# A hybrid decoder layer on one core: memory's square sums five chunks later, mix-out's first three blocks in turn by halves, token sums of x dropped between uses

## The chip, the cores and the metric

The kernel runs on one core of a Trainium2 chip. The metric is device time in microseconds (us), the median of several executions. One more execution was profiled; every trace number in this document is from such a profiled execution, counted from the start of its span.

Engines are named as in the profile: PE is TensorE (matmul), PEld its weight load, DVE is VectorE, ACT is ScalarE, POOL is GpSimd, and SP is SyncE, whose queue issues all large loads and all transposes by DMA.

## The reference, cut to what matters

One decoder layer over 256 tokens of width 2048, in float32. Two token mixers run side by side and are merged with sigmoid gates; then come cross-attention to 256 memory tokens, a gated FFN with a short convolution, and a final norm.

```python
hn = rmsnorm(h, norm_mix_w)
q, k, v, g_ret, xr, yr, g_a, g_b = split(hn @ w_in)
ret = head_groupnorm(chunkwise_retention(rotary(q), rotary(k) * dk**-0.5, v))
ret_out = silu(g_ret) * ret
hr = rg_lru(causal_dwconv(xr))                    # gates from two block-diagonal products
rnn_out = gelu(yr) * hr
merged = sigmoid(g_a) * (ret_out @ w_proj_ret) + sigmoid(g_b) * (rnn_out @ w_proj_rnn)
h = h + merged @ w_mix_out
mem_n = rmsnorm(mem, norm_mem_w)
h = h + cross_attention(rmsnorm(h, norm_xa_w), mem_n)
h = h + (silu(gate) * val) @ ffn_w_down           # gate, val = conv(rmsnorm(h, norm_ffn_w) @ ffn_w_up)
return rmsnorm(h, final_norm_w)
```

## The kernel before

**Products in two parts.** Each float32 operand is split into a high part `hi` (rounded for TensorE's fast float32 kind) and a low part `lo`. A product takes three matmuls: high by high, low by high, high by low. All are issued on L245, so the profile has one line for every matmul and tells them apart by their tiles: `acc` and `sm` are PSUM tiles (three of two banks and two of one bank), `s` is a split pair of 256 tokens, `ts` are token sums (below), `rp` the parts of the recurrence's gate products.

**Weights as one stream.** All weights lie in one array `wall`, in the order in which the kernel uses them. `weight_plan` lists the products, `pieces` cuts each into chunks, and `weight_stream` sets the order of the chunks. An ordinary product of 512 columns (`steps_n`) has chunks of 4 x 128 rows, 24 matmuls each. `prefetch` loads a chunk (1 MB) into one of three `raw` buffers, ScalarE casts its `hi` (L343), VectorE subtracts for `lo` (L344), each 1024 columns at a time, into six buffers of each kind: parts of three ordinary chunks. In the program's order the parts of two chunks ahead are made before a chunk's matmuls.

**Pairs with seven products.** `steps_pair` makes two blocks of 512 columns at once, in chunks of 2 x 128 rows by 1024 columns. An ordinary chunk has 24 matmuls. In the chunks named by `seven` (chunks 2 and 5, unless told otherwise), a scheme of seven products in place of eight takes 21 matmuls; it needs four additions of weights on VectorE (L364), seven parts in place of eight, and sums of the tokens' blocks (`sums_of`, tile `ts`). These sums are kept in the dictionary `token_sums` and used again when the same tokens meet another pair. A sum holds one of the 29 buffers of the pool `big` from its making to its last use. `SEVEN` is the default pair of chunks; `SEVEN_O` and `SEVEN_U` are other choices.

**Deferred work.** `later(n, fn)` runs `fn` in the program's order after n + 1 more chunks. `by_dma(rows, then, wait)` turns token rows into feature rows: ScalarE copies the rows into planes `pl` (L546), the SP queue issues two transposes into `pt` (L547), and after `wait` chunks ScalarE joins them into `f` (L559) and calls `then`.

**Order.** A scheduler orders each engine's instructions by priority and by when it expects buffers of a pool to be free; an engine then works through its own list in order. Matmuls are pinned to the program's order, and so are the square sums in `sum_squares` (L634).

**The stages that the change touches**, in order of time:

1. Two groups of heads: queries, keys, values and the retention gate. In the second group the values are one pair, `both("w_in", O_V + 1024)`, then the gate pair.
2. Four blocks of the recurrence, each a product for x and one for y. `recur` makes two gate products into PSUM tiles `sm` and empties them with two tanh (L889, L890); the second writes into `ti`, a buffer of `big`. `gelu_y` makes rnn's features, splits them (L582, L583) and, for features 2 and 5, makes their token sums at once from the unsplit source (L448 to L456).
3. The merge: two ordinary products for the second gate, a pair of `w_proj_rnn`, a pair for the gate, a pair of `w_proj_rnn`, then the first gate's pairs and those of `w_proj_ret`. Each merged block of 512 features goes through `by_dma` and `turn_merged` into two split pairs of the list `merged` (8 in all).
4. Mix-out (`residual`): four ordinary products `w_mix_out`, 16 chunks, each over all of `merged`. The rows of x (`hrow`) and of memory (`mnat`), eight loads of half a megabyte, are issued ahead of it. Blocks 0 and 1 run three chunks each, then the last chunk of each, then block 2, then block 3. `memory_steps` puts the four square sums of memory after the first four chunks.
5. Keys and queries of the cross-attention.

```python
def in_turn(products):
    return [c for o in products for c in o[:-1]] + [o[-1] for o in products]
```

Of the kernel before, what the change touches and what calls it, by code (L numbers as in the profile page):

```python
# [17 lines left out]
P = 128  # L18
D = 2048
S = 256  # L20
NT = D // P
# [7 lines left out]
BW = 512  # L29
KC = 4  # L30
# [11 lines left out]
SEVEN = (2, 5)  # L42
SEVEN_O = (3, 5)
SEVEN_U = (4,)

O_Q, O_K, O_V, O_G = 0, 1024, 2048, 4096
O_XR, O_YR, O_GA, O_GB = 6144, 8192, 10240, 12288
# [26 lines left out]
def weight_plan():  # L74

    plan = []
    for g in range(2):
        keys = [("w_in", 0, NT, c + g * BW) for c in (O_Q, O_K)]
        values = [("w_in", 0, NT, O_V + b * BW) for b in range(2)]
        plan += keys + [both("w_in", O_V + 1024)] if g else [keys[0], values[0], keys[1], values[1]]  # L80
        plan.append(both("w_in", O_G + g * 1024))
    for b in range(4):
        plan += [("w_in", 0, NT, c + b * BW) for c in (O_XR, O_YR)]
    plan += [("w_in", 0, NT, O_GB + b * BW) for b in range(2)] + [both("w_proj_rnn", 0)]
    plan += [both("w_in", O_GB + 1024), both("w_proj_rnn", 1024)]
    plan += [both(w, c + b * BW) for w, c in (("w_in", O_GA), ("w_proj_ret", 0)) for b in (0, 2)]
    plan += [("w_mix_out", 0, NT, b * BW) for b in range(4)]
    plan += [(w, 0, NT, b * BW) for b in range(4) for w in ("xa_w_k", "xa_w_q")]
    plan += [("xa_w_v", 0, NT, b * BW) for b in range(4)]
    plan += [both("xa_w_o", 0, SEVEN_O)] + [("xa_w_o", 0, NT, b * BW) for b in (2, 3)]  # L90
    for kind, *a in ff_plan():
        if kind == "down" and sum(a) < NF // 4:
            plan += [both("ffn_w_down", b * BW, SEVEN, a[0] * BW, 4 * a[1]) for b in (0, 2)]
        elif kind == "down":
            plan += [("ffn_w_down", a[0] * BW, 4 * a[1], b * BW) for b in range(4)]
        else:
            plan.append(both("ffn_w_up", a[0] * BW, SEVEN_U, apart=FF))
    return plan
# [28 lines left out]
    return [c for o in products for c in o[:-1]] + [o[-1] for o in products]  # L127


def weight_stream():  # L130

    out = [
        [(w, row + k * P, n, (*c[:2], k // KH in c[2]) if isinstance(c, tuple) else c) for k, n in pieces(i, nk, c)]
        for i, (w, row, nk, c) in enumerate(weight_plan())
    ]
    out[:2] = [[one for pair in zip(*out[:2]) for one in pair]]
    out[-4:-1] = [in_turn(out[-4:-1])]
    i = [c[0][0] for c in out].index("w_mix_out")
    out[i : i + 2] = [in_turn(out[i : i + 2])]
    return [one for chunks in out for one in chunks]  # L140


# [17 lines left out]
def hybrid_layer(  # L160
# [646 lines left out]
    for g in range(2):  # L807
        dec = big([P, 4, S], s="dec")
        vs, turned = [], ([], [])
        for b, o in enumerate((O_Q, O_K)):  # L810

            def rotate_both(f, o=turned[b]):
                o.append(rotated(f[:, 0:2, :]))
                later(0, lambda: o.append(rotated(f[:, 2:4, :])))

            a = gemm_n("w_in", 0, xs, NT, o + g * BW) if g + b else q0
            turned_rows(a, rs0, rotate_both, 2 - b if g + b else 3, g + b > 0)
            if b == 1:
                sp.dma_start(
                    out=dec,  # L820
                    in_=consts[:, C_DEC + g * 4 * S : C_DEC + (g + 1) * 4 * S].rearrange("p (h s) -> p h s", s=S),
                )
            if g == 0:
                v = gemm_n("w_in", 0, xs, NT, O_V + b * BW) if b else ended(v_steps)
                vs.append(split_rows(v, rs0))
        if g == 1:
            vs += [split_rows(v, rs0) for v in pair("w_in", 0, xs, NT, O_V + 1024, O_V + 1024 + BW)]
        qr, kr = turned
        gates = []
        c = O_G + g * 1024  # L830
        for a in pair("w_in", 0, xs, NT, c, c + BW):
            t = big([P, 2, BW], s="gate")
            for tt in range(2):
                act.activation(t[:, tt, :], a[:, tt, :], AF.Tanh, scale=half_rs0[:, tt : tt + 1])
            dve.scalar_tensor_tensor(out=a, in0=t, scalar=1.0, in1=a, op0=ALU.add, op1=ALU.mult)
            gates.append(a)
        retain(g, qr, kr, vs, dec, gates)


    lam = pb[:, 0:16]  # L840
# [70 lines left out]
    for b in range(4):  # L911
        rgw = big([P, 2, 4, P], s="rgw")
        for i, src in enumerate((rg_w_a, rg_w_x)):
            sp.dma_start(out=rgw[:, i], in_=src[0, 4 * b : 4 * b + 4].rearrange("g i j -> i g j"))
        xr, wparts = {}, []
        later(2, lambda wparts=wparts, rgw=rgw: wparts.extend(parts_of(rgw, pool.tensor_copy, pool)))

        def conv_x(f, b=b, xr=xr, wparts=wparts):
            xr[0] = big([P, 4, S], s="xr")
            for j in range(4):  # L920
                t = 4 * b + j
                z, y = f[:, j, :], xr[0][:, j, :]
                act.activation(y, z, AF.Identity, scale=p_cw(3, t), bias=p_cb(t))
                for s in range(1, 4):
                    dve.scalar_tensor_tensor(  # L925
                        out=y[:, s:S], in0=z[:, 0 : S - s], scalar=p_cw(3 - s, t), in1=y[:, s:S],
                        op0=ALU.mult, op1=ALU.add,
                    )

            three, xparts = [], parts_of(xr[0], act.copy, dve)  # L930

            def both(pr):
                if pr == 0:
                    three.extend(big([P, 4, S], s=n) for n in ("aa", "tt", "ti"))
                recur(b, wparts, xparts, xr[0], pr, *three)

            for pr in range(2):
                later(RG_WAIT + pr, lambda pr=pr: both(pr))

        def gelu_y(f, xr=xr):  # L940
            for pr in range(2):
                y = f[:, 2 * pr : 2 * pr + 2, :]
                y2, th = tmp("y2"), tmp("yt")
                act.activation(y2, y, AF.Square)
                dve.tensor_scalar(out=y2, in0=y2, scalar1=0.044715 * K0, scalar2=K0, op0=ALU.mult, op1=ALU.add)
                dve.tensor_tensor(out=y2, in0=y2, in1=y, op=ALU.mult)
                act.activation(th, y2, AF.Tanh)
                dve.scalar_tensor_tensor(out=y, in0=th, scalar=1.0, in1=y, op0=ALU.add, op1=ALU.mult)
            for pr in range(2):
                o = tmp("rn")  # L950
                cs = slice(2 * pr, 2 * pr + 2)
                dve.tensor_tensor(out=o, in0=xr[0][:, cs, :], in1=f[:, cs, :], op=ALU.mult)
                with_sums(rnn, SEVEN, o, 0.5)

        turned_rows(gemm_n("w_in", 0, xs, NT, O_XR + b * BW), rs0, conv_x)
        turned_rows(gemm_n("w_in", 0, xs, NT, O_YR + b * BW), rs0, gelu_y, 6)


# [11 lines left out]
        for pr in range(2):  # L970
            merged.append(split_pair(f[:, 2 * pr : 2 * pr + 2, :], 0.5))

    ts = [tanh_rows(big([P, 2, BW], s="sig"), gemm_n("w_in", 0, xs, NT, O_GB + b * BW)) for b in range(2)]
    mb = []
    for b in (0, 2):
        if b:
            ts = [tanh_rows(a, a) for a in pair("w_in", 0, xs, NT, O_GB + b * BW, O_GB + (b + 1) * BW)]
# [8 lines left out]
    for b in (0, 2):  # L986
        for i, m in enumerate(pair("w_proj_ret", 0, ret, NT, b * BW, (b + 1) * BW)):
            gated(ts[b + i], m)
            dve.tensor_add(m, m, mb[b + i])  # L989
            by_dma(m, turn_merged, 1 + 2 * (b + i == 3))  # L990


    hrow = [load_rows(x, c) for c in range(4)]
# [3 lines left out]
    def residual(w, st, out, wcol, steps=None):  # L997

        ss = sums()
        products = [steps_n(w, 0, st, NT, b * BW) for b in range(4)]  # L1000
        sources = []
        for b in range(4):
            if steps:
                steps(b)
                if b == 0:
                    for one in products[:2]:
                        for _ in range(NT // KC - 1):
                            next(one)
            elif b == 0:
                sources += pair(w, 0, st, NT, 0, BW, SEVEN_O)  # L1010
            h = hrow[b]
            dve.tensor_add(h, h, sources.pop(0) if sources else ended(products[b]))
            by_dma(h, lambda f, b=b: turn(f, b, out, wcol), 1 + (b == 1), b == 3 and steps is None)
            if b < 2:
                later(2 + b, lambda h=h, b=b: squares(h, ss, b))
            else:
                squares(h, ss, b)
        return ss
# [15 lines left out]
    def memory_steps(b):  # L1034
        if b == 0:
            ss = sums()[:, :, 0:2]
            for c in range(4):
                later(c, lambda c=c: sum_squares(mnat[c], ss, c))
            later(4, lambda: rsms.append(rstd_rows(ss)))
        if b == 2:  # L1040
            ms.load(2)
            for k2 in range(4):
# [257 lines left out]
```

## Time and profile before

| | before |
|---|---|
| time, median of 3 runs | 2010.1 us (2009.51 to 2012.91) |
| profiled execution: time, span | 2011.37 us, 2009.4 us |
| TensorE busy | 1971.7 us |
| VectorE busy | 1564.5 us |
| ScalarE busy | 1370.1 us |
| mean granted TensorE clock | 0.993 |
| read from HBM | 388.39 MB, 194 GB/s over the span |

A busy engine in the page is one that executes; its wait for a semaphore counts as idle. The view of waits names, for each line, what ended the idle time before it. A timeline merges neighbouring instructions of one kind: start, time from the first start to the last end, count, and in brackets the idle time before. A row of the windows view gives a stretch, its length, and the busy time of each engine with the count of its instructions; then come the granted TensorE clock, the share of the DMA engines and the rate in GB/s.

### The profile page before, as it was taken

Reading aid. Unit: us, or ns where it says so; the run is one execution under the profiler, and the core shown is the slowest. Engines: PE = TensorE matmul, PEld = TensorE weight load, DVE = VectorE, ACT = ScalarE, POOL = GpSimd, SP = SyncE. Lnnn points to the kernel's source line nnn. Section 1 sums busy time; section 2 is a strip of 40 time slices with the busy share of each in tenths; the row PEclk is TensorE's granted clock in tenths of the full one; section 3 lists DMA queues with packets and bytes.
Section 4 is the critical chain, followed back from the end, with each engine's and each line's share of the span. In section 5 each row is a group of like instructions: output and inputs, shape, how many; then the busy total and the mean of one; then the engine's idle time right before and its main releaser. Section 6 shows DMA issues by size and latency. Waiting matters only on the chain.

```text
span 2009.4 us, 24019 instructions
## 1 busy us (share of the span) xinstructions
PE 1971.7 (98%) x8831; PEld 1635.7 (81%) x8831; DVE 1564.5 (78%) x2044; ACT 1370.1 (68%) x1671; POOL 25.4 (1%) x25
## 2 busy tenths in 40 slices
PE   9999999998999999699999999999999999999998
PEld 8888788887888888588888888888888888888887
DVE  6887987898788888557546568678889868899686
ACT  6666658987645656568666666877877477874683
POOL 0000001000000000000000000000000000000000
PEclk9999999999999999899999999999999999999999
DMA  8756566666465465868666665756666656666673
GB/s 329 234 212 176 207 223 199 199 202 206 169 229 189 170 228 189 272 209 255 216 199 210 198 194 200 235 199 212 208 223 212 235 189 218 204 223 223 221 238 119
DMA packets 197190, 425.62 MB, mean 212 GB/s; under 512 B 142032, under 2 KB 146640, under 8 KB 152016
## 3 DMA queue, kind: packets, MB, share of 16 engines
q1 hardware_dynamic: 197072, 424.09, 63.2%
q8 instruction: 69, 1.13, 0.2%
q14 instruction: 49, 0.40, 0.1%
HBM read 388.39 MB, written 2.10 MB: 194 GB/s over the span
## 4 chain that ended last, share of the span: by engine, by line
PE 92%; DVE 3%; ACT 2%; issue 1%; DMA 1%; SPq 0%; POOL 0%; POOLq 0%; DVEq 0%; ACTq 0%
PE acc L245 67%; PE sm L245 25%; DVE lo L344 1%; ACT hi L343 1%; ACT f L559 0%; DMA nat<-in_mem 0%; ACT pl L546 0%; DVE tb L728 0%; DVE xr L925 0%; PE warm L242 0%; DVE rows L572 0%; DMA pt<-pl 0%; DVE ta L732 0%; DVE raw L364 0%; DVE fv L1127 0%
## 5 line engine op out<-in xcount | busy, mean ns | idle before, releaser
L245 PE MATMUL acc<-hi,s 128*128 128x512 f32 (+1 forms) x3974 | 1221.9, 389 | 17.2 <-ACT s L582 17.1
L344 DVE TENSOR_TENSOR lo<-raw,hi 128x1024 fp32r<-128x1024 f32 (+1 forms) x796 | 933.4, 1197 | 337.2 <-ACT hi L343 328.4
L343 ACT CAST hi<-raw 128x1024 fp32r<-128x1024 f32 (+1 forms) x796 | 792.4, 1023 | 419.0 <-PE acc L245 145.5
L245 PEld LDWEIGHTS acc<-hi,s 128*128 128x128 f32 x3974 | 745.5, 188 | 170.5 <-ACT s L582 17.6
L245 PE MATMUL acc<-lo,s 128*128 128x512 f32 (+1 forms) x1987 | 772.1, 389 | 1.7 <-DVE lo L344 1.7
L245 PEld LDWEIGHTS acc<-lo,s 128*128 128x128 f32 x1987 | 374.1, 188 | 79.4 <-DVE lo L344 2.5
L245 PE MATMUL sm<-hi,s 128*128 128x512 f32 x1336 | 411.3, 389 | 0.0
L245 PEld LDWEIGHTS sm<-hi,s 128*128 128x128 f32 x1336 | 250.8, 188 | 52.0
L245 PE MATMUL sm<-lo,s 128*128 128x512 f32 x668 | 260.0, 389 | 0.0
L559 ACT COPY f<-pt 128x1024 uint16<-128x1024 uint16 x128 | 167.0, 1353 | 35.5 <-DMA pt<-pl 33.9
L245 PEld LDWEIGHTS sm<-lo,s 128*128 128x128 f32 x668 | 125.4, 188 | 26.0
L364 DVE TENSOR_TENSOR raw<-raw 128x512 f32<-128x512 f32 x164 | 113.1, 690 | 2.5
L245 PE MATMUL acc<-hi,ts 128*128 128x512 f32 x246 | 76.8, 394 | 1.4 <-ACT hi L343 1.4
L546 ACT COPY pl<-rows 128x1024 uint16<-128x1024 uint16 x56 | 55.7, 1042 | 21.6 <-DVE rows L570 12.2
L546 ACT COPY pl<-o 128x1024 uint16<-128x1024 uint16 x52 | 51.6, 1039 | 6.4 <-DVE o L989 6.4
L245 PEld LDWEIGHTS acc<-hi,ts 128*128 128x128 f32 x246 | 46.3, 189 | 11.7 <-ACT hi L343 2.2
L245 PE MATMUL acc<-lo,ts 128*128 128x512 f32 x123 | 49.0, 398 | 1.1 <-DVE lo L344 1.1
L1127 DVE SCALAR_TENSOR_TENSOR fv<-f,pf,fv 128x255 f32<-128x255 f32 (+1 forms) x88 | 38.6, 482 | 0.0
L524 DVE TENSOR_TENSOR o<-o,acc 128x512 f32<-128x512 f32 x52 | 33.4, 687 | 6.1 <-PE acc L245 6.1
L1127 DVE SCALAR_TENSOR_TENSOR fg<-f,pf,fg 128x255 f32<-128x255 f32 (+1 forms) x88 | 35.8, 479 | 0.0
L514 DVE TENSOR_TENSOR o<-o,acc 128x512 f32<-128x512 f32 x52 | 35.6, 685 | 0.0
L524 DVE TENSOR_TENSOR o<-o,sm 128x512 f32<-128x512 f32 x52 | 34.4, 688 | 0.3 <-PE sm L245 0.2
(193 smaller groups left out, 1011.1 us busy)
## 6 DMA issues: line engine op xcount, KB each, us to landing
raw<-in_wall SPq DMA_DIRECT2D x352, 1024.0 KB, 4.8
nat<-in_x SPq DMA_DIRECT2D x8, 512.0 KB, 9.2
raw<-in_wall SPq DMA_DIRECT2D x7, 512.0 KB, 5.9
pt<-pl SPq DMA_TRANSPOSE x128, 3.3
nat<-in_mem SPq DMA_DIRECT2D x4, 512.0 KB, 8.8
xt<-in_x_t SPq DMA_DIRECT2D x3, 512.0 KB, 8.9
xt<-in_mem_t SPq DMA_DIRECT2D x3, 512.0 KB, 5.5
dec<-in_consts SPq DMA_DIRECT2D x2, 512.0 KB, 4.4
```

Source lines behind the costliest of these rows:

```text
L245: tc.keep_in_program_order(pe.matmul(*a, **k))
L343: act.copy(hi[:, cs], src[:, cs])
L344: dve.tensor_tensor(out=lo[:, cs], in0=src[:, cs], in1=hi[:, cs].bitcast(F32), op=ALU.subtract)
L364: dve.tensor_tensor(out=o, in0=a, in1=b, op=ALU.add)
L514: dve.tensor_tensor(out=o, in0=a, in1=b, op=op)
L524: dve.tensor_tensor(out=o, in0=o, in1=banks[a], op=ALU.add)
L546: act.copy(planes[:, tt], words[:, tt])
L559: act.copy(halves_[:, :, :, cs], turned_[:, :, :, cs])
L1127: dve.scalar_tensor_tensor(out=y[:, s:S], in0=z[:, j, 0 : S - s], scalar=pf[:, 2 - s, t : t + 1], in1=y[:, s:S], op0=ALU.mult, op1=ALU.add,)
```

## The change

- `SEVEN_V = (5,)`: the second group's value pair uses the seven-product scheme in chunk 5 alone. Chunk 2 becomes an ordinary chunk.
- `token_sums.clear()` after the two groups of heads: the sums of x made there are not kept; the gate pairs of the merge make them again.
- `gelu_y` only splits. The token sums of features 2 and 5 of rnn are made by `later` after the first of the merge's ordinary gate products, from the split parts (one more addition each).
- Mix-out's blocks 0, 1 and 2 run two chunks each, then their other two chunks each (`by_halves`); block 3 follows as before. The weight stream is laid out in the same order.
- The fourth merged block is joined one chunk earlier.
- Memory's square sums come after chunks 6 to 9 in place of 1 to 4, and their root after chunk 10.

```diff
+SEVEN_V = (5,)
...
-        plan += keys + [both("w_in", O_V + 1024)] if g else [keys[0], values[0], keys[1], values[1]]
+        plan += keys + [both("w_in", O_V + 1024, SEVEN_V)] if g else [keys[0], values[0], keys[1], values[1]]
...
+def by_halves(products):
+
+    return [c for part in (slice(0, 2), slice(2, 4)) for o in products for c in o[part]]
...
-    out[i : i + 2] = [in_turn(out[i : i + 2])]
+    out[i : i + 3] = [by_halves(out[i : i + 3])]
...
-            vs += [split_rows(v, rs0) for v in pair("w_in", 0, xs, NT, O_V + 1024, O_V + 1024 + BW)]
+            vs += [split_rows(v, rs0) for v in pair("w_in", 0, xs, NT, O_V + 1024, O_V + 1024 + BW, SEVEN_V)]
...
+    token_sums.clear()
...
-                with_sums(rnn, SEVEN, o, 0.5)
+                rnn.append(split_pair(o, 0.5))
...
-    ts = [tanh_rows(big([P, 2, BW], s="sig"), gemm_n("w_in", 0, xs, NT, O_GB + b * BW)) for b in range(2)]
-    mb = []
+    ts, mb = [], []
+    for b in range(2):
+        ts.append(tanh_rows(big([P, 2, BW], s="sig"), gemm_n("w_in", 0, xs, NT, O_GB + b * BW)))
+        if b == 0:
+            for i, k2 in enumerate(SEVEN):
+                later(1 + 2 * i, lambda k2=k2: sums_of(rnn[k2]))
...
-            by_dma(m, turn_merged, 1 + 2 * (b + i == 3))
+            by_dma(m, turn_merged, 1 + (b + i == 3))
...
-                    for one in products[:2]:
-                        for _ in range(NT // KC - 1):
+                    for one in products[:3]:
+                        for _ in range(2):
                             next(one)
...
-                later(c, lambda c=c: sum_squares(mnat[c], ss, c))
-            later(4, lambda: rsms.append(rstd_rows(ss)))
+                later(5 + c, lambda c=c: sum_squares(mnat[c], ss, c))
+            later(9, lambda: rsms.append(rstd_rows(ss)))
```

## The prediction

> **What bounds the kernel now.** I read the page first, then what TensorE waits for, then the stages around its waits as timelines.
>
> ```profile
> span 2009.4 us, 24019 instructions
> PE 1971.7 (98%) x8831; PEld 1635.7 (81%) x8831; DVE 1564.5 (78%) x2044; ACT 1370.1 (68%) x1671; POOL 25.4 (1%) x25
> PE 92%; DVE 3%; ACT 2%; issue 1%; DMA 1%; SPq 0%; POOL 0%; POOLq 0%; DVEq 0%; ACTq 0%
> ...
> L344 DVE TENSOR_TENSOR lo<-raw,hi 128x1024 fp32r<-128x1024 f32 (+1 forms) x796 | 933.4, 1197 | 337.2 <-ACT hi L343 328.4
> L343 ACT CAST hi<-raw 128x1024 fp32r<-128x1024 f32 (+1 forms) x796 | 792.4, 1023 | 419.0 <-PE acc L245 145.5
> ...
> L364 DVE TENSOR_TENSOR raw<-raw 128x512 f32<-128x512 f32 x164 | 113.1, 690 | 2.5
> ```
>
> TensorE carries 92% of the chain that ended last and is idle for only 2009.4 - 1971.7 = 37.7 us. Work taken off another engine is worth something only if it closes one of those holes, or the slow stretch behind it. This is the list of the holes:
>
> ```profile
> PE acc L245 <- ACT s L582: 17.1, 1, 17.1
> PE sm L245 <- ACT ti L890: 8.1, 2, 6.6
> PE acc L245 <- DVE lo L344: 2.8, 4, 1.0
> PE acc L245 <- ACT hi L343: 1.4, 1, 1.4
> ```
>
> One wait of 17.1 us, two on L890 and five small ones. The change touches the places of the first two rows, and of part of the others.
>
> **Mix-out (first part of the change).** Here are TensorE's stretch before the hole (chain of waits), its first matmuls behind it (timeline) and the stretch that they begin (chain), then ScalarE and the SP queue over the same time.
>
> ```profile
> 817.60 10.67 PE acc L245 x47
> ...
> 845.62 1.52 PE L245 MATMUL acc<-hi,s 128*128 128x512 f32 x2 [17.14 <-ACT s L582]
> ...
> 845.62 59.52 PE acc L245 x251
> ```
>
> ```profile
> 828.34 1.04 ACT L343 CAST hi<-raw 128x1024 fp32r<-128x1024 f32 x1 [0.32 <-PE acc L245]
> 841.36 1.06 ACT L634 ACTIVATE nat<-nat 128x1024 f32<-128x1024 f32 x1 [11.97 <-DMA nat<-in_mem]
> ...
> 842.41 2.50 ACT L559 COPY f<-pt 128x1024 uint16<-128x1024 uint16 x2
> 844.94 1.15 ACT L582 ACTIVATE s<-f 128x512 fp32r<-128x512 f32 x2
> ```
>
> ```profile
> 825.52 0.40 SPq L216 DMA_DIRECT2D raw<-in_wall  x1
> 826.02 5.04 SPq L547 DMA_TRANSPOSE pt<-pl  x2
> 831.12 2.11 SPq L212 DMA_DIRECT2D nat<-in_x  x4
> 833.33 2.35 SPq L216 DMA_DIRECT2D nat<-in_mem  x4
> 835.78 36.71 SPq L216 DMA_DIRECT2D raw<-in_wall  x6
> ...
> DMA to landing us min/median/max: 8.0/9.6/13.0
> ```
>
> A mix-out chunk is 24 matmuls. 10.67 / 47 = 0.227 us each, so 5.45 us a chunk. TensorE did two chunks of block 0 (merged pairs 0 to 3), then needed pair 4. Its turned rows were to be copied and split by ScalarE, but the pinned square sum of memory (L634) stood ahead and waited 11.97 us for its load, which is the fifth of eight half-megabyte loads issued at 831 to 836. The hole ends when L634, the two copies (2.50) and the split (1.15) are done.
>
> After the change two things hold. By the instruction order that the changed program builds to, no L634 stands ahead of the copies: the four come after the casts of the tenth to twelfth chunks. And TensorE has six chunks (two of each of three blocks) that need pairs 0 to 3 alone: 6 x 5.45 = 32.7, from 817.6 to 850.3.
>
> When are pairs 4 to 7 there? ScalarE's next two instructions are now the casts of the sixth chunk. They wait for the buffers of the third, whose first half is free after 18 of 24 matmuls: 828.3 + 4.1 = 832.4, the second at 833.8; the cast ends by 834.8. Its weights were issued at 825.52, ahead of the eight loads. Then come two copies and two splits, twice: 2 x (2.50 + 1.15) = 7.3, so 842.1, and about 1.3 more for VectorE's low parts: 843.4, 7 us before need.
>
> What is late next is the seventh chunk's weights, queued behind the eight loads. They are issued at 835.78 and land at most 13.0 later (last row above): 848.8. Cast and subtraction (1023 and 1197 ns, L343 and L344) end at 851.0, while TensorE wants the high part at 850.3 and the low part 0.45 later. That leaves 0 to 0.4 us of waiting; I take 0.4.
>
> The stretch behind the hole is slow at its start: its 251 matmuls take 59.52 us where 251 x 0.227 = 57.0, so 2.5 more. The stage can give 17.1 + 2.5 = 19.6; I take **-19.2**. The square sums now fall among the casts of chunks 10 to 12, where ScalarE has room or not (a rival below). They issue no DMA, and the loads keep their places in the SP queue. What waits for the sums, the scaling of the first key block, comes after mix-out.
>
> **Recurrence (token sums dropped, sums of rnn later).**
>
> ```profile
> 478.48 1.60 PE L245 MATMUL sm<-rp,rp 128*128 128x256 f32 x12
> ...
> 492.13 2.93 PE L245 MATMUL sm<-rp,rp 128*128 128x256 f32 x12 [6.58 <-ACT ti L890]
> ```
>
> ```profile
> 482.82 0.64 ACT L455 ACTIVATE ts<-tq 128x512 fp32r<-128x512 f32 x1 [2.77 <-DVE tq L450]
> ...
> 485.02 1.98 ACT L546 COPY pl<-rows 128x1024 uint16<-128x1024 uint16 x2
> 486.91 1.99 ACT L343 CAST hi<-raw 128x1024 fp32r<-128x1024 f32 x2
> 491.60 0.84 ACT L890 ACTIVATE ti<-sm,h 128x256 f32<-128x256 f32 x2 [2.71 <-DMA pt<-pl]
> ...
> 480.70 0.42 DVE L448 TENSOR_TENSOR tq<-rn 128x256 f32<-128x256 f32 x1
> ...
> 483.84 1.40 DVE L572 TENSOR_SCALAR rows<-acc,ro 128x512 f32<-128x512 f32 x2
> 485.16 0.68 DVE L456 SCALAR_TENSOR_TENSOR ts<-tq,ts 128x512 fp32r<-128x512 f32 x1
> ```
>
> The second gate product pair needs the PSUM tiles that L889 and L890 empty. L890 waited for a transpose: its output `ti` is one of the 29 buffers of the pool `big`, all taken, and the next one to come free was the planes that the transpose reads. Dropping x's token sums after the second head group gives back two of the 29 for all four recurrence blocks, and the sums of rnn 2 and 5 are not yet made, which is one more in the third block and two in the fourth. In the built order of the changed program the fourth block's `ti` waits for no DMA. The four VectorE steps of the sum and L455 go too, so the rows of L572 start near 479.6 instead of 483.84. ScalarE's planes follow (2.0), then two casts (2.0) and the two tanh pairs (1.7): from 480.3 they end at 486.0, the first PSUM tile free near 485.2. TensorE wants it at 485.4. The hole gives 6.58, the half-speed products 2.93 - 1.60 = 1.33, the matmuls after them 0.2. The other hole on this line is 8.1 - 6.6 = 1.5 us in the third block, where ScalarE waited for the same kind of sum. Together 9.6; I take **-9.1**, with 0.5 left over.
>
> **V pair of the second head group (SEVEN_V).**
>
> ```profile
> 200.19 0.50 PE L245 MATMUL acc<-lo,ts 128*128 128x512 f32 x1 [0.53 <-DVE lo L344]
> 217.09 0.73 PE L245 MATMUL acc<-hi,ts 128*128 128x512 f32 x2 [1.42 <-ACT hi L343]
> 218.34 0.50 PE L245 MATMUL acc<-lo,ts 128*128 128x512 f32 x1 [0.53 <-DVE lo L344]
> ...
> 198.00:223.00 25.00, 22.53 (x89) 17.16 (x88) 23.64 (x35) 20.89 (x23) 0.00 (x0) 0.93 0.46 157
> ```
>
> Chunk 2 becomes an ordinary one: 24 matmuls instead of 21, so 3 x 0.227 = +0.7 on the path. VectorE, busy 23.64 of 25 us here, loses four additions (4 x 0.69) and one and a half subtractions of L344 (1.8); ScalarE as many casts (1.5). The first hole goes. The second needs chunk 5's additions 2 us earlier, and 4.6 us of VectorE's work ahead of them has gone. Best case: 0.53 + 1.42 + 0.53 of waiting and the lower clock, 7% of 25 = 1.75, less 0.7: -3.5. Worst case: nothing closes, +0.7. It lies nearer to the first; I take **-2.9**.
>
> The clock gate's rule weighs on this term alone. "TensorE: Matmul & The Clock Gate" of the Trainium skill, section "What's actually happening", has the clock fall to half after an idle window of about 3.4 us. No hole here is that long, so by the page these 1.75 us are no consequence of the holes and would stay: the sum would be 1.7 us smaller. The row shows 0.93 around holes of 1.42 us at most, so I follow the row.
>
> **Merge.** Two sums of x are made again (an addition, three short steps and a subtraction: 0.69 + 0.42 + 0.29 + 0.29 + 0.68 = 2.4 each, the two 0.29 an estimate from L448 at half size), and each sum of rnn gets an addition, since its source is gone. That is 2 x 2.4 + 2 x 0.69 = 6.2 us of VectorE between 500 and 570:
>
> ```profile
> 520.00:530.00 10.00, 10.00 (x45) 8.27 (x45) 9.71 (x14) 6.39 (x9) 0.00 (x0) 1.00 0.29 105
> 550.00:560.00 10.00, 10.00 (x46) 8.29 (x45) 9.43 (x10) 6.52 (x7) 0.00 (x0) 1.00 0.78 287
> 580.00:620.00 40.00, 40.00 (x178) 33.12 (x177) 30.62 (x36) 20.89 (x24) 0.00 (x0) 1.00 0.55 203
> ```
>
> The cover is the parts that are made two chunks ahead; TensorE has no hole here. With VectorE at 9.7 of 10 the cover is thin. Bounds: 0 and the full 6.2; the rows show TensorE unbroken at this load, so I take **+0.5**.
>
> **Sum.** -19.2 - 9.1 - 2.9 + 0.5 = -30.7. The profiled execution took 2011.37 us, its span and 2.0 around it, and lies 1.3 above the median of 2010.1. From the median: 2010.1 - 30.7 = 1979.4.
>
> **Rivals.**
>
> *ScalarE becomes late in mix-out.* Three blocks now end 11 us apart, so their planes, joins, splits and squares crowd into the time of ten chunks, 54.5 us, together with the memory's square sums.
>
> ```profile
> 845.60:924.00 78.40, 78.38 (x335) 64.45 (x336) 45.34 (x56) 59.01 (x82) 0.70 (x1) 0.97 0.66 214
> ```
>
> ScalarE was busy 59.0 us in this stretch; less the 7.3 for the merged pairs, 52 remain for 54.5. It decides at the casts of chunks 13 to 17: each us they come later than I think beyond some 3 to 5 us of lead is lost. For it: the in-order queue waits for transposes in between. Against it: part of the 52 may fall after mix-out. Price up to 8: 1979.4 + 8 = 1987. Chance 0.15.
>
> *VectorE is late in the merge*: the full 6.2 and a slow stretch of 2: 1979.4 + 7.7 = 1987. Chance 0.08.
>
> *The change does not do what it says in the recurrence*: another tile of `big` takes the freed buffers and the hole stays: 1979.4 + 9.1 = 1988.5. For it: the pool has been full. Against it: the built order has no such wait. Chance 0.07.
>
> *Slower: the granted clock falls once TensorE is never idle.* Place: the whole span, 1972 us of busy TensorE. Price: 19.7 us for each 1% of mean clock, now 0.993. The saving is eaten at 0.977, and the time is over 2014 below 0.975. For it: nothing but that a longer unbroken load has not been seen. Against it: the 40 us from 580 at full load show 1.00. Time at 0.97: 2025. Chance 0.03.
>
> **How the numbers follow.** The forecast has 0.67. Its own range is the sum with every term at its best, 19.6 + 9.6 + 3.5 = 32.7, so 1977, and a little below it for the small holes in the FFN; upward, the V pair giving nothing, 1983. The three rivals of 1987 to 1988.5 bring the high end to 1989; the low end is 1975. Left out: the slower case and two rivals together. What a measurement of this kernel tells from no change is about 0.2%, 4 us. Only if two large terms fail is the gain under that, so: faster 0.95, within 0.2% 0.02, slower 0.03.
>
> **What would show it.** Right: no wait on L582 over 1 us, TensorE unbroken for six chunks in mix-out; no wait of `sm` on the tanh over 1 us; ScalarE's first memory square without idle time before it. Wrong: a new wait on casts late in mix-out (first rival), on subtractions in the merge (second), on the tanh in the fourth block (third), or a clock below 0.99. The whole is wrong if the 17.1 us turn up as another wait of the same size.

## The result, and the profile after

| | before | changed |
|---|---|---|
| time, median of 4 runs each, on one chip | 2011.51 us (2009.51 to 2013.43) | 1982.45 us (1980.76 to 1984.39) |
| profiled execution: time, span | 2011.37, 2009.4 us | 1980.76, 1979.0 us |

The ratio is 0.9856, 95% interval 0.9839 to 0.9873: faster, by 29.1 us between the medians and 30.6 between the profiled executions, where 30.7 was forecast. The predicted time of 1979.4 is 3.1 below the median and within the range. The page of the changed kernel:

```profile
span 1979.0 us, 24013 instructions
PE 1965.8 (99%) x8834; PEld 1631.4 (82%) x8834; DVE 1564.5 (79%) x2050; ACT 1367.1 (69%) x1671; POOL 26.8 (1%) x25
```

TensorE's idle time went from 37.7 to 1979.0 - 1965.8 = 13.2 us; VectorE and ScalarE are as busy as before. What TensorE still waits for (in total, times, longest; most lines named above have moved down by six, L889 and L890 by seven):

```profile
PE acc L251 <- DVE lo L350: 2.6, 5, 0.8
PE sm L251 <- DVE o L530: 1.6, 2, 1.4
PE warm L248 <- DVE half L1183: 1.1, 1, 1.1
PE sm L251 <- ACT ti L897: 0.3, 1, 0.3
```

The 17.1 us on the split are gone, the 8.1 on the second tanh are 0.3, and one row is new: 1.6 us on L530, the additions that empty the last PSUM banks of a seven-product pair.

The two traces are matched by counting matmuls (behind chunk 2 of the value pair the changed kernel has three more); the table gives the start of the same matmul in both, in us:

| the matmul | before | changed | difference | this stage |
|---|---|---|---|---|
| ahead of the value pair | 197.02 | 196.50 | -0.51 | start-up -0.5 |
| just behind the value pair | 226.22 | 222.42 | -3.81 | value pair -3.3 |
| early in the gate pair behind it | 240.05 | 238.46 | -1.59 | new wait +2.2 |
| behind the fourth block's hole | 500.10 | 488.60 | -11.51 | recurrence -9.9 |
| start of mix-out | 817.66 | 806.15 | -11.51 | merge 0.0 |
| behind mix-out's hole | 870.07 | 838.79 | -31.27 | mix-out -19.8 |
| end of mix-out | 926.06 | 895.32 | -30.73 | seventh chunk +0.5 |
| last matmul | 2002.00 | 1971.47 | -30.53 | the rest +0.2 |

**Mix-out.** The windows row of its first six chunks (us; busy time of PE, PEld, DVE, ACT, POOL with counts; clock; DMA share; GB/s), then ScalarE's timeline:

```profile
806.00:839.00 33.00, 33.00 (x147) 27.16 (x145) 18.85 (x20) 20.12 (x21) 0.00 (x0) 1.00 0.93 304
```

```profile
822.22 1.05 ACT L349 CAST hi<-raw 128x1024 fp32r<-128x1024 f32 x1 [0.26 <-PE acc L251]
823.18 2.56 ACT L565 COPY f<-pt 128x1024 uint16<-128x1024 uint16 x2
825.77 1.15 ACT L588 ACTIVATE s<-f 128x512 fp32r<-128x512 f32 x2
826.83 2.55 ACT L565 COPY f<-pt 128x1024 uint16<-128x1024 uint16 x2
829.41 1.15 ACT L588 ACTIVATE s<-f 128x512 fp32r<-128x512 f32 x2
837.07 2.00 ACT L349 CAST hi<-raw 128x1024 fp32r<-128x1024 f32 x2 [6.50 <-DMA raw<-in_wall]
```

TensorE runs through 33 us without a gap. ScalarE goes from the sixth chunk's cast straight to the copies and splits; merged pairs 4 to 7 are split at 830.6 and, with VectorE's low parts, ready at 831.4; TensorE wants them at 838.8. ScalarE then waits 6.5 us for that chunk's weights.

**Recurrence.** ScalarE, then TensorE at the fourth block's second gate products (timelines):

```profile
476.87 2.00 ACT L552 COPY pl<-rows 128x1024 uint16<-128x1024 uint16 x2 [1.16 <-DVE rows L578]
478.77 2.00 ACT L349 CAST hi<-raw 128x1024 fp32r<-128x1024 f32 x2
480.67 0.46 ACT L896 ACTIVATE tr<-sm,h 128x256 f32<-128x256 f32 x1
481.04 0.45 ACT L897 ACTIVATE ti<-sm,h 128x256 f32<-128x256 f32 x1
```

```profile
482.15 1.59 PE L251 MATMUL sm<-rp,rp 128*128 128x256 f32 x12
```

No wait stands before the tanh, and the twelve matmuls take 1.59 us at full clock, against 2.93 behind the old hole.

**The new wait.** VectorE's timeline ahead of the gate pair:

```profile
229.62 0.16 DVE L863 TENSOR_SCALAR lt<-lt 128x16 f32<-128x16 f32 x1
229.69 1.22 DVE L350 TENSOR_TENSOR lo<-raw,hi 128x1024 fp32r<-128x1024 f32 x1
230.83 0.17 DVE L862 TENSOR_TENSOR lt<-lt 128x16 f32<-128x16 f32 x1
...
231.75 1.28 DVE L530 TENSOR_TENSOR o<-o,acc 128x512 f32<-128x512 f32 x2
232.94 0.68 DVE L530 TENSOR_TENSOR o<-o,sm 128x512 f32<-128x512 f32 x1
233.54 1.41 DVE L601 SCALAR_TENSOR_TENSOR v<-o,ro,v 128x512 fp32r<-128x512 f32 x2
234.86 0.68 DVE L530 TENSOR_TENSOR o<-o,sm 128x512 f32<-128x512 f32 x1
```

The gate pair's `sm` banks are free when the two `sm` additions are done. TensorE, which now leaves the value pair earlier, waits for the first until 233.6 and for the second until 235.5. Ahead of them stand a weight's low part and small steps on `lt`, the polynomial of the recurrence's rates (L854 to L866), which the scheduler puts here now.

### The profile page after: what moved, and what is told of

Read it like the earlier page. It is cut to its first block, busy times and chain, and to the rows that moved or that the text cites. A ratio compares the mean times of both kernels' runs of the same rounds, so it can differ in the third digit from the quotient of the medians.

```text
span 1979.0 us, 24013 instructions
## 1 busy us (share of the span) xinstructions
PE 1965.8 (99%) x8834; PEld 1631.4 (82%) x8834; DVE 1564.5 (79%) x2050; ACT 1367.1 (69%) x1671; POOL 26.8 (1%) x25
## 4 chain that ended last, share of the span: by engine, by line
PE 91%; DVE 3%; ACT 3%; issue 1%; DMA 1%; SPq 0%; POOL 0%; POOLq 0%; DVEq 0%; ACTq 0%
PE acc L251 66%; PE sm L251 25%; DVE lo L350 1%; DMA raw<-in_wall 1%; ACT hi L349 1%; ACT f L565 1%; ACT pl L552 0%; DMA pt<-pl 0%; DVE xr L932 0%; DVE tb L734 0%; ACT rows L804 0%; DMA raw<-in_head 0%; DVE fv L1138 0%; DVE o L530 0%; DVE raw L370 0%
## 5 line engine op out<-in xcount | busy, mean ns | idle before, releaser
L552 ACT COPY pl<-rows 128x1024 uint16<-128x1024 uint16 x56 | 55.7, 1042 | 24.8 <-DVE rows L576 13.3
L530 DVE TENSOR_TENSOR o<-o,acc 128x512 f32<-128x512 f32 x52 | 33.2, 678 | 5.7 <-PE acc L251 5.7
L530 DVE TENSOR_TENSOR o<-o,sm 128x512 f32<-128x512 f32 x52 | 33.9, 677 | 0.1
```

The lines of the kernel that those rows point to most:

```text
L530: dve.tensor_tensor(out=o, in0=o, in1=banks[a], op=ALU.add)
L552: act.copy(planes[:, tt], words[:, tt])
```

## Experiments

Each time has its ratio to the kernel before, run on the same chip.

**Mix-out: which edit closes the hole?** Theory A: the pinned square sums, waiting for their load, made it. Theory B: the order of the chunks. First, the kernel before with the later square sums alone:

```diff
-                later(c, lambda c=c: sum_squares(mnat[c], ss, c))
-            later(4, lambda: rsms.append(rstd_rows(ss)))
+                later(5 + c, lambda c=c: sum_squares(mnat[c], ss, c))
+            later(9, lambda: rsms.append(rstd_rows(ss)))
```

> The kernel before with one edit: memory's square sums after chunks 6 to 9 of mix-out. The order of the chunks stays as before, so TensorE has four chunks (two of block 0, then of block 1 its first two) before it needs merged pair 4... in the old order it needs pair 4 after two chunks (from 828.5 on). Theory A (the pinned square sums, waiting 11.97 us for their load, made the hole): ScalarE goes from the casts straight to the copies, the first split ends near 833 to 834.5, so the hole shrinks from 17.1 to 4.7 to 6 us, the gain is 11 to 14 us, time 1996 to 1999. Theory B (the order of the chunks made the hole, and the square sums only stood beside it): the hole stays above 10 us and the gain is under 7.

1997.08 us, 0.9931 (0.9919 to 0.9944). In the list of waits the row is now

```profile
PE acc L245 <- ACT s L582: 4.0, 1, 4.0
```

The hole shrank much as theory A has it (4.7 to 6 us were expected to stay). Then the order alone:

```diff
+    return [c for part in (slice(0, 2), slice(2, 4)) for o in products for c in o[part]]
...
-    out[i : i + 2] = [in_turn(out[i : i + 2])]
+    out[i : i + 3] = [by_halves(out[i : i + 3])]
```

> The kernel before with one edit: mix-out's blocks 0, 1 and 2 in turn by halves, the weight stream in the same order; the square sums stay after chunks 1 to 4. Theory A (the square sums made the hole): ScalarE still stands in them until about 841 to 842, and the merged pairs 4 to 7 are split from 845 on, but now TensorE has six chunks, until 850, if its weights come. The casts of the later chunks stand behind the square sums too, so a wait of 2 to 8 us remains, on casts or on the split; gain 9 to 16. Theory B (the order alone is enough): no wait over 1 us in mix-out, gain 18 to 20, and the square sums' move is worth nothing.

1993.32 us, 0.9913 (0.9899 to 0.9926). ScalarE in the timeline, and TensorE's wait:

```profile
841.11 1.06 ACT L639 ACTIVATE nat<-nat 128x1024 f32<-128x1024 f32 x1 [6.71 <-DMA nat<-in_mem]
...
842.16 2.53 ACT L564 COPY f<-pt 128x1024 uint16<-128x1024 uint16 x2
844.73 1.15 ACT L587 ACTIVATE s<-f 128x512 fp32r<-128x512 f32 x2
...
849.95 1.98 ACT L348 CAST hi<-raw 128x1024 fp32r<-128x1024 f32 x2
```

```profile
PE acc L250 <- ACT hi L348: 2.6, 2, 1.4
```

ScalarE still stands in the square sum until 841, but TensorE has work meanwhile; a cast behind two square sums makes it wait 1.2 us. Over mix-out, by matched matmuls, the square sums alone give 13.3 us, the order alone 17.5, both 19.2 (19.7 in a second profile). Neither theory of this run held as it stood: the gain of 17.7 us is above A's range, and B's "no wait over 1 us" failed. Either edit would have had most of the stage's gain; the rest adds 1.7 to 2.2 once the order is changed. The rest is the square sums and the stage's third edit, the fourth merged block joined one chunk earlier, which was in neither of these runs and was not run alone.

**Recurrence: freed buffers, or the work of the sums?** The kernel before with rnn's sums later, and nothing else:

```diff
-                with_sums(rnn, SEVEN, o, 0.5)
+                rnn.append(split_pair(o, 0.5))
...
+        if b == 0:
+            for i, k2 in enumerate(SEVEN):
+                later(1 + 2 * i, lambda k2=k2: sums_of(rnn[k2]))
```

> The kernel before with one edit: the token sums of rnn are made in the merge from the split parts; x's token sums stay in their buffers. It tells apart what closed the hole of 6.6 us before the fourth block's gate products. Theory A (the prediction: buffers of the pool are what the second tanh waits for, and x's two sums hold two of them): without the two freed buffers the tanh still waits, for a transpose; the hole stays above 3 us, the gain is 1 to 5. Theory B (the four steps of the sum on VectorE, and the split's ScalarE steps, made the planes late): the hole falls under 1 us and the gain is 8 to 10, as with both edits.

2001.16 us, 0.9954 (0.9941 to 0.9966). The kernel before with `token_sums.clear()` alone:

> The kernel before with one edit: the dictionary of x's token sums is emptied after the head groups, so the merge makes them again; rnn's sums stay in the recurrence. Theory A (buffers): the tanh of the fourth block finds a free buffer, the wait on it goes from 6.6 to under 2 us, the gain is 5 to 9. Theory B (the work of rnn's sums): the hole stays above 4 us and the gain is under 3. Should e3 and e4 each close it, either alone is enough; should neither, both are needed.

2004.58 us, 0.9969 (0.9956 to 0.9981). The kernel before with a larger pool, paid for by temporaries:

```diff
-    bp = ctx.enter_context(tc.tile_pool(name="bp", bufs=29))
-    tp = ctx.enter_context(tc.tile_pool(name="tp", bufs=10))
+    bp = ctx.enter_context(tc.tile_pool(name="bp", bufs=30))
+    tp = ctx.enter_context(tc.tile_pool(name="tp", bufs=8))
```

> The kernel before with 30 buffers in place of 29 in the pool of large tiles, paid for by two of the ten small temporary ones; nothing else is changed, so x's and rnn's token sums stay where they were. Theory A (the second tanh of the fourth block waits for a buffer of this pool): one more buffer is enough, the wait of 6.6 us before the fourth block's gate products falls to 1 to 2 us (what stays is ScalarE's wait for the sum of rnn), the hole of 1.5 us in the third block stays, gain 4 to 7 us, 2004 to 2007. Theory B (the wait is set by VectorE's sums ahead of the planes alone): the wait stays above 4 us, gain under 2.

2005.56 us, 0.9962 (0.9950 to 0.9975). ScalarE and TensorE at the fourth block with the emptied dictionary alone (timelines):

```profile
481.10 0.63 ACT L455 ACTIVATE ts<-tq 128x512 fp32r<-128x512 f32 x1 [2.76 <-DVE tq L450]
...
483.30 1.99 ACT L546 COPY pl<-rows 128x1024 uint16<-128x1024 uint16 x2
485.18 0.85 ACT L891 ACTIVATE ti<-sm,h 128x256 f32<-128x256 f32 x2
```

```profile
485.72 1.69 PE L245 MATMUL sm<-rp,rp 128*128 128x256 f32 x12 [1.27 <-ACT ti L891]
```

The tanh no longer waits for a transpose, and the hole is 1.27 us in place of 6.58; what stays is ScalarE's wait of 2.76 us for rnn's sum. One buffer more does the same (hole 1.72). From just ahead of the third block's hole to 500 us, both give 6.7 us. Later sums alone give 10.1, as much as the whole change: they too free a buffer by the fourth block, and they remove the work, which also closes the 1.5 us of the third block.

So the tanh did wait for a buffer; but my expectation of the first of these runs was wrong in holding that x's two buffers are needed. The changed kernel without the emptied dictionary says the same:

> The changed kernel with one part undone: x's token sums stay in their two buffers between uses. Theory A (in the recurrence it is enough that rnn's sums come later, as the run with that edit alone showed; the emptied dictionary adds nothing): no wait on the second tanh over 0.5 us, the merge makes two sums fewer, and the time is that of the changed kernel within 0.5 us. Theory B (with the other edits in, the two buffers are needed): a wait of 2 us or more in the third or fourth block, 2 to 7 us slower.

1983.8 us, 0.9866 (0.9851 to 0.9881), beside 1981.66, 0.9858 (0.9843 to 0.9873), for the changed kernel on the same chip. The recurrence gains the same 10.1 us. In the recurrence the emptied dictionary adds nothing. Beside the second profile of the changed kernel (below), this one falls behind by 1.7 us at mix-out's seventh chunk and by 2.0 later. Two profiles of the changed kernel differ by only 0.5 us at such places, but the other version that keeps the sums (below) loses nothing at the seventh chunk. Both versions have medians about 2 us above the changed kernel's on this chip, with overlapping intervals, so whether the emptied dictionary helps outside the recurrence stays open.

**Value pair: what is it worth?** The changed kernel with `SEVEN_V = SEVEN`:

> The changed kernel with one part undone: the second head group's value pair has seven products in both of its chunks again. Theory A (the part is worth about 1.1 us net: it closes 3 us of holes in the pair, but VectorE, with time on its hands there, takes the small polynomial of the recurrence's rates ahead of the additions that empty the value pair, and TensorE waits 1.6 us for them at the gate pair): the holes of 0.5, 1.4 and 0.5 us are back, the wait on those additions is gone, 0.5 to 1.5 us slower than the changed kernel, so 1983 to 1984. Theory B (the wait at the gate pair has nothing to do with this part): it stays, and the kernel is 2.5 to 3.5 us slower than the changed one, 1985 to 1986. The slow-clock matmuls behind the second hole were seen in two profiles of four with this code and not in the others; they are 1.6 us either way.

1981.45 us, 0.9845 (0.9832 to 0.9858): by its ratio no slower than the changed kernel. TensorE and the window of the prediction, in this run:

```profile
217.06 0.73 PE L251 MATMUL acc<-hi,ts 128*128 128x512 f32 x2 [1.39 <-ACT hi L349]
218.32 0.50 PE L251 MATMUL acc<-lo,ts 128*128 128x512 f32 x1 [0.53 <-DVE lo L350]
...
220.46 0.50 PE L251 MATMUL acc<-lo,ts 128*128 128x512 f32 x1 [0.47 <-DVE lo L350]
```

```profile
198.00:223.00 25.00, 22.09 (x93) 16.73 (x92) 23.66 (x35) 20.89 (x23) 0.00 (x0) 1.00 0.47 158
```

The holes are back and the wait on L530 is gone, so the part does cause that wait. But the clock is 1.00 with the holes there. Seven profiles have the value pair with both seven-product chunks; two show matmuls of 0.43 us behind the second hole, five do not, and those five pass this stretch 0.85 us sooner than the kernel before. The changed kernel passes it 1.08 sooner, 0.95 in a second profile. So against an execution at full clock the part is worth 0.1 to 0.2 us. Why the clock fell in two of the seven is taken up in the last section.

**Is it the polynomial?** The changed kernel with L852 to L871 in a function that `later(0, rates)` runs:

> The changed kernel with one edit: the polynomial of the recurrence's rates comes by deferral after the gate pair's first chunk has begun, so in the built order of VectorE it stands behind the additions that empty the value pair. Theory A (the polynomial holds up these additions, and so TensorE): the wait on the additions at the gate pair (1.6 us in two pieces, 2.2 with the matmuls behind it) falls under 0.3 us; 1.5 to 2.2 us faster than the changed kernel, about 1980.5. Theory B (the value parts for the products to come, made on VectorE in the same stretch, hold them up): the wait stays above 1 us and the time is the same, about 1982.5.

1980.96 us, 0.9845 (0.9831 to 0.9858). The wait stayed, in one piece:

```profile
PE sm L251 <- DVE o L530: 1.3, 1, 1.3
```

The polynomial was out of the way and the first `sm` addition came at 231.80 in place of 232.94, but TensorE was 1.0 us earlier too, and VectorE had no idle time since 226. Theory A's mechanism was a part of the cause only: the stretch gained 1.5 us, of it half in the pair itself. Then I moved the work itself, with `SEVEN_V = (2,)`:

> The changed kernel with one edit: the value pair of the second head group has its seven products in chunk 2 in place of chunk 5, so VectorE's four additions of weights and the four that empty the finished PSUM banks come some 15 us earlier; the amount of work on every engine is the same. Theory A (TensorE waits 1.6 us at the gate pair because VectorE's work of chunk 5 stands close ahead of the additions that empty the pair): that wait falls under 0.3 us, the holes of chunk 5 (0.14 and 0.48) go, one or two of about 0.5 come at chunk 2; 1.0 to 2.2 us faster than the changed kernel. Theory B (VectorE, busy 38.8 of 42 us, is the bound of the whole stretch, wherever its work stands): the wait stays above 1 us or the same sum of holes turns up at chunk 2; within 0.5 us of the changed kernel.

1981.0 us, 0.9853 (0.9839 to 0.9868), beside 1981.66 for the changed kernel. The waits of TensorE that are left there, in the timeline:

```profile
214.73 0.50 PE L251 MATMUL acc<-lo,s 128*128 128x512 f32 x1 [0.87 <-DVE lo L350]
```

The wait on L530 is gone from the list; 0.53 us at chunk 2 and these 0.87 took its place. The stretch is 0.9 to 1.0 us shorter than in the changed kernel. I read this as VectorE's backlog: from 198 to 240 it is busy 38.8 of 42 us in the changed kernel, and 37.8 in the run with the deferred polynomial, whose stretch is 1.5 us shorter. TensorE's wait moves with the place of that work. By time, no version is told apart from the changed kernel.

**The seventh chunk's weights.** With the deferred polynomial, and memory's four loads spread among the weight loads:

> The changed kernel with the rates' polynomial deferred as in the run before, and memory's four loads spread among the weight loads of mix-out's chunks in place of standing in a row ahead of the seventh chunk's weights. Theory A (the seventh chunk's weights are late because of the eight loads ahead of them): the wait on its low part (0.25 us, with the slow matmuls 0.5) goes, no other comes in mix-out; 0.3 to 0.6 us below the run with the polynomial alone, about 1980. Theory B (HBM traffic as a whole makes them late): the wait stays or moves to the eighth or ninth chunk, same time or up to 1 us slower.

1985.21 us, 0.9864 (0.9849 to 0.9879). In mix-out the seventh chunk's weights landed at 830.2, against 835.5 in the run with the polynomial alone, and no wait is left. That these loads cost the 0.5 us is not shown by it: the changed kernel's second profile (below) has the eight loads in a row and no wait there either. In the FFN this run lost 4.0 us against the kernel before; TensorE's timeline shows where most of them went, and the chain of waits what came before, first in this run, then in the run with the polynomial alone:

```profile
1457.74 0.73 PE L251 MATMUL acc<-hi,ts 128*128 128x512 f32 x2 [1.64 <-ACT hi L349]
1459.34 0.79 PE L251 MATMUL acc<-lo,ts 128*128 128x512 f32 x1 [0.87 <-DVE lo L350]
```

```profile
1438.32 8.73 DMA pt<-pl
```

```profile
1438.77 6.41 DMA pt<-pl
```

The chain runs over a transpose that ScalarE's join waits for. It took 8.7 us to land in place of 6.4, and the 1 MB of weights issued just ahead of it 8.3 in place of 5.7, though ScalarE's instructions there stand in the same order. Why it hits this kernel stays open. The kernel with `SEVEN_V = (2,)` and kept sums, meant as the best version, met it too (8.6 us for the transpose):

> The changed kernel with both edits: seven products in chunk 2 of the value pair, and x's token sums kept. Theory A of both: 1.0 to 2.5 us faster than the changed kernel, 1980 to 1981.5; it would be the fastest version. Theory B of either: the same or slower.

1983.45 us, 0.9862 (0.9846 to 0.9879). The changed kernel once more, for the comparisons above:

> The changed kernel itself, on the same chip as the three others, so that tenths of a per cent can be compared. Expected: 1982.5, ratio to the kernel before 0.985 to 0.987. A second profile of it also tells whether TensorE ever falls to the slower clock around 220 us in this kernel: if that clock depends on the holes, no; if it depends on when the execution began, it may be there, beside a start-up that stays slow until about 7 us.

Its second profile repeats the first to 0.1 us up to mix-out; it has no wait at the seventh chunk (0.5 us in the first) and no slow clock around 220 us. By itself it does not settle the question put to it, since its start-up was fast as well; the last section does, from all profiles.

## Why the prediction was right, point by point

- **Mix-out, -19.2 forecast, -19.2 measured** (-19.7 in the second profile). The steps held one by one. The cast ended ahead of the copies; the first square sum of memory starts at 848.72 with no idle time before it, as was named as a sign; the pairs were ready 7.4 us before need where 7 was said; late next were the seventh chunk's weights, behind the eight loads, with a first wait of 0.25 us and 0.3 of matmuls spaced wider behind it, where 0 to 0.4 was said. The chain of waits (start, length, what) has the load; it took 12.0 us where 13.0 at most was assumed:

```profile
824.93 12.04 DMA raw<-in_wall
...
839.43 119.52 PE acc L251 x526
```

- **Recurrence, -9.1 forecast, -9.9 measured.** The wait for a pool buffer is shown by the run with 30 buffers. I took the two buffers of x's sums as part of the cause; later sums alone suffice. I kept 0.5 in hand, and none was needed: each PSUM tile was free 0.7 us before TensorE needed it.
- **Value pair, -2.9 forecast, -1.1 between these two profiles, 0.1 to 0.2 like for like.** This term was mis-sized, in two steps. I took the low clock of one execution as the sure price of the holes, 1.75 us; five of seven profiles with the same holes have full clock, and where the clock fell it cost 0.85 us. And I closed the holes without saying what is late next. The pair gained 3.3 us, that is 2.5 beyond the 0.85 (one hole, 0.48 us, stayed); then VectorE had to empty the pair's banks, and 2.2 us came back at the gate pair. No rival named that wait. The Trainium skill, "TensorE: Matmul & The Clock Gate", section "What's actually happening", has free-running windows of about 3.4 us, so that one kernel differs between executions; the traces agree with that (a step of 3.41 us, last section). Its rule that a whole idle window comes first does not explain the two executions with a slow stretch, whose holes are 1.4 and 0.5 us. Following the row was right in this: the low clock did come from the holes.
- **Merge, +0.5 forecast, 0.0 measured.** Part of the new sums lie in this stretch; VectorE is full there, and TensorE has no gap:

```profile
550.00:560.00 10.00, 10.00 (x46) 8.26 (x45) 9.97 (x16) 3.15 (x4) 0.00 (x0) 1.00 0.31 108
```

- **Not forecast:** -0.5 us at start-up, which comes and goes between executions.
- **The rivals.** ScalarE late in mix-out, VectorE late in the merge, a hole left in the recurrence, a lower clock: none came. From 839 to 895, where the first was to show, ScalarE is busy 51.4 of 56.0 us, and TensorE's only gap is the 0.25 us named above. The mean clock rose to 0.999.
- **The time.** The sum fits the profiled executions to 0.1 us, and that is luck: the value pair gave 1.8 us less than forecast, while the recurrence gave 0.8, the merge 0.5 and the start-up 0.5 more. The median lies 1.7 above its own fastest run of four, the profiled one; executions of the changed kernel spread over 3.6 us.

## What to carry to other kernels

When a wait is closed, ask what the waiting engine needs next from the engine that was late: here the closed holes were worth 2.5 us at full clock, and 2.2 of them came back at the next use of PSUM banks that VectorE has to empty. Before two remedies for one hole are added up, price each alone: in mix-out they give 13.3 and 17.5 us and together 19.2, in the recurrence one alone gives everything. A slow-clock stretch behind short holes in a single profile is not a sure term of a sum: here two of seven profiles had it.

## What the runs showed of the hardware

TensorE's clock behind a hole. After 17 us the matmuls were slow for 3.4 to 6 us. After 4.05 us (the run with later square sums, timeline) the first slow one came after 0.7 us, and they stayed slow until 834.9:

```profile
830.68 0.49 PE L245 MATMUL acc<-hi,s 128*128 128x512 f32 x1 [4.05 <-ACT s L582]
831.40 0.69 PE L245 MATMUL acc<-hi,s 128*128 128x512 f32 x1 [0.23 <-DVE s L583]
831.89 0.63 PE L245 MATMUL acc<-lo,s 128*128 128x512 f32 x1
832.32 1.05 PE L245 MATMUL acc<-hi,s 128*128 128x512 f32 x2
```

After single holes of 1.27 to 1.72 us in the recurrence they were not (1.69 to 1.70 us for the twelve matmuls). A hole of 1.4 to 1.6 us and one of 0.5 to 0.9, with 0.7 us between them, gave a slow stretch in four profiles (two at the value pair, both of those seen in the FFN) and none in five.

The times at which the clock changes tell these apart. In each of the fourteen profiles, from the first change to full clock up to the last matmul, it changes only at multiples of 3.41 us behind that first change; in the kernel before at 218.85, 222.26, 488.50, 495.33, 833.25 and 850.31. These multiples cut a profile into windows. Twelve windows at full clock have 1.78 us or more of TensorE's idle time, and behind each the next window is at half clock. In all others at full clock the idle time is at most 1.72 us, and none is followed by half clock. Here are the windows with the value pair's holes and the one behind them (rows of the windows view), first in the kernel before, then in the changed kernel with both seven-product chunks back:

```profile
215.43:218.85 3.42, 1.47 (x6) 0.76 (x5) 3.11 (x8) 3.42 (x5) 0.00 (x0) 1.00 0.00 0
218.85:222.26 3.41, 3.41 (x9) 2.52 (x9) 3.38 (x7) 3.00 (x5) 0.00 (x0) 0.50 0.25 38
```

```profile
212.87:216.28 3.41, 2.80 (x13) 1.99 (x11) 3.38 (x9) 3.26 (x4) 0.00 (x0) 1.00 0.00 0
216.28:219.69 3.41, 2.10 (x8) 1.34 (x8) 3.12 (x9) 3.41 (x5) 0.00 (x0) 1.00 0.00 0
219.69:223.11 3.42, 2.96 (x14) 2.19 (x13) 3.42 (x4) 2.76 (x4) 0.00 (x0) 1.00 0.51 127
```

In the kernel before both holes lie in one window, idle 3.42 - 1.47 = 1.95 us; in the other run a boundary at 216.28 parts them, 0.61 and 1.31 us. So the holes made the low clock in the profiled execution of the kernel before, and it was chance that they fell into one window.
